# A two-block transformer kernel: stick-breaking sums by a VectorE scan, moved modulations, new allowances

## The chip, the cores and the metric

The kernel runs on one core of a Trainium2 chip. The metric is the device time of one execution in microseconds (us), the median over several runs. Names of engines: PE is TensorE (matrix products and transposes), PEld its weight loads, DVE is VectorE, ACT is ScalarE, POOL is GpSimd, SP is SyncE, whose queue issues the DMA transfers.

## The reference

Two blocks act on x (512 x 1024, fp32). Block 1 puts 16 meta tokens ahead of x, normalises, multiplies by w_in, runs a causal pooling over windows of 2, 4, 8 and 16 tokens and a forgetting attention of 8 heads, merges the two with gates and adds the product with w_out. Block 2 takes c through w_ada to six vectors of 1024 (the modulations: shift, scale and gate of each half), then attention and an MLP. Its attention has 8 stick-breaking heads and 8 chunked heads with relative positions:

```
z = q k^T / 8                         # 128 queries, all keys up to them
strict = s_idx < t_idx
log_1m_beta = where(strict, log_sigmoid(-z), 0)
suffix = cumsum(log_1m_beta, axis=keys, reverse=True) - log_1m_beta
w = where(strict, exp(log_sigmoid(z) + suffix), 0)
out = w @ v
...
mod = silu(c) @ w_ada + b_ada         # sh1, sc1, gt1, sh2, sc2, gt2
x = x + gt1 * (mixed @ w_o)
x = x + gt2 * (square(relu(h @ w1)) @ w2)
```

So the weight of key s for query t is exp(z minus the sum, over keys s to t-1, of softplus(z)).

## The kernel before

Products are made from fp32r parts: each operand is split into a high part (ACT cast, L131) and a low rest (DVE or POOL subtraction, L128), and mm3 (L149 to L152) issues three matmuls for one product. Tiles of weights are 512 KB, loaded raw by SP's queue into the tag wr (5 buffers) and split.

The order of PE's work is set when the program is written. Attention and dense products are generators; weave runs them against each other by a model clock clk and shares of it (SHARE1, SHARE2). After a step, mark or at sets when its result may be used; the allowance is a LAT_ constant in model ns. Other engines follow a scheduler that keeps the written order where data allow it.

The stages, in us of the profiled span: opening with first_norm and the first v products, 0 to 45; weave 1 (attn1 beside dense1: pooling with u_tile at L540 to L565, up-products in ups), 45 to 330; w_out with two joint_norm calls (L711 on) that normalise twice, 330 to 425; the first q, k and v of block 2; the second attention (attn2 beside dense2: v2_chunk, q and k of the pairs, first half of w_o), 443 to 672; the rest of w_o and the norm, to 745; the first MLP half w1 (L1200 to L1308), to 874; the second, w2, to 1055.

The six modulations are made by ada (L203): eight loads of 512 KB each and 16 DVE operations (L215 the first, L217 the rest) that accumulate 128 partial sums. todo holds those still to come, ada_step takes one, and ada_all (L655) takes what is left after weave 1. Modulation 5 is made in the loop of w2, ft 2 to 9.

attn2 goes through pairs of heads in ORDER; p below 4 is a stick-breaking pair, handled by sb_steps with **keys on partitions**: first makes z for one tile of 128 keys and adds a bf16 mask product (L944), then ACT does Abs, Exp, Ln (L946 to L948), DVE does max and addition, giving softplus (L949), a cast (L950) and the rest (L951). second (L963) lets PE add the sums over later keys: a product with the constant ntri (minus ones in a triangle) or nones (minus ones) for each later key tile and for both parts, into the PSUM bank of z. ACT's Exp (L965) gives the weights for pv2 (L916). The chunked pairs, ca_steps, have **queries on partitions**: soft-max on ACT and DVE, PE transposes in turn (L1002), and copies out of PSUM by ACT (L1005) or DVE (L1007) by turns.

```
d0 = min(128 * j2, 256)
pe.matmul(ps[:, d0:], ntri if j2 == j else nones, part[:, SOFF[j2]:SOFF[j2] + 512 - d0],
          start=False, stop=part is sl and j2 == j, skip_group_check=True)
```

Of the kernel before, what the change touches and what calls it, by code (L numbers as in the profile page):

```python
# [51 lines left out]
def hybrid_then_adaln_block(ctx, tc, a, out, tap=None):  # L52
# [96 lines left out]
    def mm3(ps, lh, ll, rh, rl, start, stop):  # L149
        pe.matmul(ps, lh, rh, start=start, stop=False)  # L150
        pe.matmul(ps, lh, rl, start=False, stop=False)  # L151
        pe.matmul(ps, ll, rh, start=False, stop=stop)  # L152
# [1268 lines left out]
```

## Time and profile before

| what | value |
|---|---|
| median of 3 runs | 1059.36 us (1059.28 to 1059.82) |
| profiled execution | 1057.35 us, its span 1055.2 us, mean granted clock 0.994 |
| PE busy | 96% of the span, 5918 instructions |
| DVE, ACT, POOL busy | 60%, 53%, 29% |
| PE stick-breaking sums (L963) | 2% of the chain that ended last |
| DMA | 125.54 MB, 119 GB/s |

The profile is one execution seen by the hardware profiler. Its page gives the busy time of each engine, the waits with what ended them, and groups of instructions by line of the kernel. A time is the start in us from the beginning of the span. A duration of PE is modelled at its end, so the pace of matmuls is read from one start to the next. The granted clock is a share of TensorE's full speed.

### The profile page before, as it was taken

The page shows a single profiled execution, that of the slowest core. Times are in us where ns is not written, and L with a number is a line of the kernel's source. Part 1 is how long each engine was busy: PE and PEld are TensorE (multiplying, and loading weights), DVE is VectorE, ACT ScalarE, POOL GpSimd, SP SyncE. Part 2 cuts the span into 40 slices and gives each one's busy share as a digit, 9 for nine tenths or more (in the row PEclk, how much of TensorE's full clock was granted, in tenths as well). Part 3 has the DMA queues.
Part 4 walks back from the last instruction along what each step waited for, and adds up shares of the span by engine and source line. Part 5 has one row for each costly group of instructions (what it writes and reads, how often), then busy time and mean ns, then how long its engine had stood idle before and what let it go on. Part 6 is the DMA issues. An engine that isn't in the chain of part 4 may idle for free.

```text
span 1055.2 us, 15524 instructions
## 1 busy us (share of the span) xinstructions
PE 1012.8 (96%) x5918; PEld 857.8 (81%) x5918; DVE 628.3 (60%) x1184; ACT 561.8 (53%) x1082; POOL 301.0 (29%) x157
## 2 busy tenths in 40 slices
PE   7999999899999999999899988999999979999998
PEld 5987977768888888987678866799999978888886
DVE  6465866764533669367777476569588862611115
ACT  6365654454545645466687686347567753222220
POOL 3322123423322543203202115122121233233330
PEclk9999999999999999999999999999999999999999
DMA  8442533454543566326421234443234334633302
GB/s 238 126 122 63 154 94 102 138 138 122 149 112 100 181 198 192 128 72 189 126 63 61 68 101 140 146 113 82 66 94 120 121 120 135 177 109 100 100 20 80
DMA packets 136059, 125.54 MB, mean 119 GB/s; under 512 B 8141, under 2 KB 112417, under 8 KB 135986
## 3 DMA queue, kind: packets, MB, share of 16 engines
q1 hardware_dynamic: 135986, 124.56, 40.6%
q8 instruction: 46, 0.75, 0.3%
q14 instruction: 27, 0.22, 0.1%
HBM read 119.82 MB, written 4.73 MB: 118 GB/s over the span
## 4 chain that ended last, share of the span: by engine, by line
PE 76%; DVE 9%; issue 5%; ACT 3%; DMA 3%; POOL 3%; SPq 0%; DVEq 0%; POOLq 0%; ACTq 0%
PE ps L150 19%; PE ps L152 18%; PE ps L151 18%; PE ps L1204 4%; PE ps L1206 3%; PE ps L1205 3%; DVE ada L217 2%; PE ps L963 2%; DMA wr<-in_w_ada_dram 2%; POOL wl L128 1%; DMA wr<-in_w_in_dram 1%; PE ps L519 1%; PE ps L438 1%; PE ps L439 1%; DVE QK L427 1%
## 5 line engine op out<-in xcount | busy, mean ns | idle before, releaser
L128 POOL TENSOR_TENSOR wl<-wr,wh 128x1024 fp32r<-128x1024 f32 x99 | 248.1, 2511 | 577.7 <-ACT wh L131 567.1
L131 ACT CAST wh<-wr 128x1024 fp32r<-128x1024 f32 x130 | 136.3, 1050 | 106.5 <-PE ps L151 55.7
L150 PE MATMUL ps<-hh,wh 128*128 128x512 f32 (+1 forms) x352 | 129.7, 368 | 0.0
L151 PE MATMUL ps<-hl,wh 128*128 128x512 f32 (+1 forms) x352 | 125.1, 355 | 0.0
L152 PE MATMUL ps<-hh,wl 128*128 128x512 f32 (+1 forms) x352 | 124.8, 355 | 0.0
L150 PE MATMUL ps<-wh,T 128*128 128x512 f32 x256 | 101.0, 394 | 0.0
L152 PE MATMUL ps<-wh,T 128*128 128x512 f32 x256 | 100.4, 392 | 0.0
L151 PE MATMUL ps<-wl,T 128*128 128x512 f32 x256 | 100.2, 391 | 0.0
L217 DVE SCALAR_TENSOR_TENSOR ada<-wr,vc,ada 128x512 f32<-128x512 f32 x84 | 81.7, 972 | 11.4 <-DMA wr<-in_w_ada_dram 10.4
L150 PEld LDWEIGHTS ps<-hh,wh 128*128 128x128 f32 x352 | 66.3, 188 | 20.4 <-issue 11.5
L152 PEld LDWEIGHTS ps<-hh,wl 128*128 128x128 f32 x352 | 66.4, 189 | 9.7
L151 PEld LDWEIGHTS ps<-hl,wh 128*128 128x128 f32 x352 | 66.4, 189 | 7.7
L128 DVE TENSOR_TENSOR wl<-wr,wh 128x1024 fp32r<-128x1024 f32 x31 | 41.4, 1336 | 29.1 <-ACT wh L131 29.1
L152 PEld LDWEIGHTS ps<-wh,T 128*128 128x128 f32 x256 | 48.1, 188 | 11.4
L151 PEld LDWEIGHTS ps<-wl,T 128*128 128x128 f32 x256 | 48.1, 188 | 10.7
L150 PEld LDWEIGHTS ps<-wh,T 128*128 128x128 f32 x256 | 48.1, 188 | 10.6
L150 PE MATMUL ps<-h2h,wh 128*128 128x512 f32 (+1 forms) x144 | 54.9, 381 | 0.0
L1206 PE MATMUL ps<-QK,wl 128*128 128x256 f32 x192 | 53.7, 280 | 0.0
L1204 PE MATMUL ps<-QK,wh 128*128 128x256 f32 x192 | 53.7, 279 | 0.0
L1205 PE MATMUL ps<-PT,wh 128*128 128x256 f32 x192 | 53.4, 278 | 0.0
L152 PE MATMUL ps<-h2h,wl 128*128 128x512 f32 (+1 forms) x144 | 53.3, 370 | 0.0
L151 PE MATMUL ps<-h2l,wh 128*128 128x512 f32 (+1 forms) x144 | 53.1, 369 | 0.0
(412 smaller groups left out, 2672.6 us busy)
## 6 DMA issues: line engine op xcount, KB each, us to landing
wr<-in_w_in_dram SPq DMA_DIRECT2D x64, 512.0 KB, 5.8
wr<-in_w_dram SPq DMA_DIRECT2D x64, 512.0 KB, 4.1
wr<-in_w_ada_dram SPq DMA_DIRECT2D x48, 512.0 KB, 4.9
wr<-in_w_out_dram SPq DMA_DIRECT2D x12, 512.0 KB, 3.5
wr<-in_w_o_dram SPq DMA_DIRECT2D x12, 512.0 KB
xr<-in_x_dram SPq DMA_DIRECT2D x8, 512.0 KB
wr<-in_w_up_pool_dram SPq DMA_DIRECT2D x8, 256.0 KB
wr<-in_w_up_attn_dram SPq DMA_DIRECT2D x8, 256.0 KB, 3.3
```

The costliest lines, as they stand in the source:

```text
L128: (eng or pool).tensor_tensor(dst, raw, f(hi), op=OP.subtract)
L131: act.copy(dst_hi, raw)
L150: pe.matmul(ps, lh, rh, start=start, stop=False)
L151: pe.matmul(ps, lh, rl, start=False, stop=False)
L152: pe.matmul(ps, ll, rh, start=False, stop=stop)
L217: dve.scalar_tensor_tensor(acc, raw[:, q, :], cs, acc, op0=OP.mult, op1=OP.add)
L427: dve.scalar_tensor_tensor(A[e][other], src[own], scale, f(A[e][own]), op0=OP.mult, op1=OP.subtract)
L438: pe.matmul(ps, A[e][:, sa], B[e][:, sb], start=True, stop=False)
L963: pe.matmul(ps[:, d0:], ntri if j2 == j else nones, part[:, SOFF[j2]:SOFF[j2] + 512 - d0], start=False, stop=part is sl and j2 == j, skip_ ...
L1204: pe.matmul(ps, wh, bh, start=first and k == 0, stop=False, **go)
L1205: pe.matmul(ps, wh, bl, start=False, stop=False, **go)
L1206: pe.matmul(ps, wl, bh, start=False, stop=k == 3, **go)
```

## The change

- Stick-breaking: sb_steps goes, and so do ntri, nones and the products at L963, the cast and the low rest. att2_steps serves both kinds of pairs with queries on partitions. stick (one unit per 128 queries i and head e, keys 128(i+1)) has the mask turned, Abs, Exp, Ln, max and addition as before, then one DVE scan backward over the keys (a reversed view of the tile; state times one plus the element), the subtraction from z, and Exp in place. Then turn: i+1 PE transposes and one copy, by ACT or DVE by turns. That makes 10 transposes and 4 copies a head.
- attn2: units of a head in the order of i, a lag of three units in place of two, allowances by size for both kinds; LAT_PV2, LAT_QK2, LAT_SQ, LAT_CA and LAT_ADA are longer. pack_a and pack_b change places for q and k.
- Modulation 4 is made in weave 1 (ada_step takes three for m of 4 and more in ups) and no longer after it. ada(5) first copies a column of hid[31], the last tile of w1's result, into its accumulator: the accumulations can only begin behind it.
- u_tile for group 3 (window 16): four additions on DVE in place of POOL.
- Opening: the row of norm_g is loaded ahead of x; 6, 4 and 6 products of ones that nobody reads are put ahead of the first ones.
- v2_chunk: four accumulations in two PSUM banks in place of four.

```
--- before.py
+++ after.py
@@ -34,14 +34,16 @@
 ORDER = (0, 1, 4, 2, 5, 3, 6, 7)
 LAST_SB = 3
 DENSE = (1, "v2", 4, 2, 5, 3, "v3", 6, 7)
-LAT_CA = 5600.0
+LAT_CA = 6000.0
 LAT_SM = 3200.0
-LAT_SB = 4000.0
-LAT_CM = 3200.0
+LAT_SB = (4000.0, 5500.0, 6500.0, 7500.0)
+LAT_CM = (3200.0, 3800.0, 4400.0, 5000.0)
 LAT_QK = 2600.0
-LAT_SQ = 3800.0
-LAT_ADA = 4000.0
+LAT_SQ = 5000.0
+LAT_ADA = 6500.0
 LAT_PV = 600.0
+LAT_PV2 = 1500.0
+LAT_QK2 = 3800.0
...
-    def ada(v, j):
+    def ada(v, j, late=None):
         half, k = j // 4, 2 * (j % 4)
         raw = wts.tile([128, 2, 512], F32, name="wr", tag="wr", bufs=5)
         x = a["w_ada_2"]
@@ -208,6 +210,8 @@
                                   ap=[[6 * D, 128], [128 * 6 * D, 2], [1, 512]]))
         if k == 0:
             ada_acc[0] = consts.tile([128, 512], F32, name="ada", tag="ada", bufs=1)
+            if late is not None:
+                dve.tensor_copy(ada_acc[0][:, :1], late)
         acc = ada_acc[0]
...
+    sp.dma_start(gn, rows(a["norm_g"], 0, 1, D, 0, D))
     sp.dma_start(xr[0], rows(a["x"], 0, 128, D, 0, D))
-    sp.dma_start(gn, rows(a["norm_g"], 0, 1, D, 0, D))
+    idle = bank()
+
+    def warm(n):
+
+        for _ in range(n):
+            pe.matmul(idle[:, :128], ones_f, ones_f, start=True, stop=True)
+
+    warm(6)
...
+    warm(4)
     load_wv(0)
     sp.dma_start(xr[1], rows(a["x"], 128, 128, D, 0, D))
     first_norm(xr[0], 128, NM, *x0)
+    warm(6)
...
         for q in range(g + 1):
             s = wt([128, NP], "T")
-            pool.tensor_tensor(s[:, 2 * w - 1:], prev[:, 2 * w - 1:], prev[:, w - 1:NP - w], op=OP.add)
+            (dve if g == 3 else pool).tensor_tensor(s[:, 2 * w - 1:], prev[:, 2 * w - 1:], prev[:, w - 1:NP - w], op=OP.add)
...
         for m in range(8):
             yield from ups(m)
-            ada_step(2)
-
-    todo += [(v, k) for v in (0, 1, 3) for k in range(8)]
+            ada_step(2 if m < 4 else 3)
+
+    todo += [(v, k) for v in (0, 1, 3, 4) for k in range(8)]
...
     weave((SHARE1, attn1()), (1.0, dense1()))
-    ada_all()
+    assert not todo
...
-    bdt = gated([128, 384], "Cm", late, F32R)
-    bd, nones, ntri = (bdt[:, 128 * q:128 * q + 128] for q in range(3))
+    bd = gated([128, 128], "Cm", late, F32R)
     dve.memset(f(bd), 0.0)
-    dve.tensor_scalar(nones, ones_f, -1.0, None, op0=OP.mult)
...
-    pool.affine_select(mk, mk, pattern=[[1, 128]], base=0, channel_multiplier=-1, compare_op=OP.is_gt, fill=NEG)
+    pool.affine_select(mk, mk, pattern=[[-1, 128]], base=0, channel_multiplier=1, compare_op=OP.is_gt, fill=NEG)
...
-        pss = [bank() for _ in range(4)]
+        pss = [b[:, 256 * q:256 * q + 256] for b in (bank(), bank()) for q in range(2)]
...
-            pack_b(*QK2[p][1:], ps, slice(0, 512), 0.125)
+            pack_a(QK2[p][0], ps, 0.125)
...
-            pack_a(QK2[p][0], ps)
+            pack_b(*QK2[p][1:], ps, slice(0, 512))
...
-            e1 = wt([128, 512], "T")
-            act.activation(e1[:, c0:], ps[:, c0:], AF.Abs)
-            act.activation(e1[:, c0:], e1[:, c0:], AF.Exp, scale=-1.0)
-            act.activation(e1[:, c0:], e1[:, c0:], AF.Ln, bias=1.0)
-            dve.scalar_tensor_tensor(e1[:, c0:], ps[:, c0:], 0.0, e1[:, c0:], op0=OP.max, op1=OP.add)
-            dve.tensor_copy(sh[:, so:so + n], e1[:, c0:])
-            dve.tensor_tensor(sl[:, so:so + n], e1[:, c0:], f(sh[:, so:so + n]), op=OP.subtract)
...
-            for part in (sh, sl):
-                for j2 in range(3, j - 1, -1):
-                    d0 = min(128 * j2, 256)
-                    t += (512 - d0) / 2.4
-                    pe.matmul(ps[:, d0:], ntri if j2 == j else nones, part[:, SOFF[j2]:SOFF[j2] + 512 - d0],
-                              start=False, stop=part is sl and j2 == j, skip_group_check=True)
-            act.activation(WT[:, WOFF[j]:WOFF[j] + n], ps[:, c0:], AF.Exp)
...
+    def att2_steps():
+        def products(p, i, e, stop):
             if i == 0:
-                st[p, e] = (None, None, wt([128, 4, 512], "PT"))
-            bs = strips[2 * (p - 4) + e]
+                st[p, e] = wt([128, 4, 512], "PT"), wt([128, 4, 512], "Y") if p < 4 else None
             L = 128 * (i + 1)
             N = max(L, 256)
             ps = bank()
-            mm_packed(ps[:, :N], QK2[p], e, slice(128 * i, 128 * i + 128), slice(0, N), True)
-            x = P[p, i, e] = wt([128, 512], "T")
+            mm_packed(ps[:, :N], QK2[p], e, slice(128 * i, 128 * i + 128), slice(0, N), stop)
+            x = P[p, i, e] = st[p, e][1][:, i, :] if p < 4 else wt([128, 512], "T")
+            return ps[:, :L], x[:, :L], 2 * N / 2.4
+
+        def stick(p, i, e):
+
+            z, x, t = products(p, i, e, False)
+            pe.matmul(z[:, 128 * i:], identb, mkb, start=False, stop=True)
+            act.activation(x, z, AF.Abs)
+            act.activation(x, x, AF.Exp, scale=-1.0)
+            act.activation(x, x, AF.Ln, bias=1.0)
+            dve.scalar_tensor_tensor(x, z, 0.0, x, op0=OP.max, op1=OP.add)
+            back = x[:, ::-1]
+            dve.tensor_tensor_scan(back, ones_f[:, :1].to_broadcast([128, z.shape[1]]), back, 0.0, op0=OP.mult, op1=OP.add)
+            dve.tensor_tensor(x, z, x, op=OP.subtract)
+            act.activation(x, x, AF.Exp)
+            return t + 56
+
...
             x = P.pop((p, i, e))
-            PT = st[p, e][2]
+            PT = st[p, e][0]
             pt = bank().rearrange("p (j n) -> p j n", j=4)
             for j in range(i + 1):
                 pe.transpose(pt[:, j, :], x[:, 128 * j:128 * j + 128], ident)
...
+        units = [(p, i, e) for p in ORDER for e in range(2) for i in range(4)]
+        LAG = 3
         ripe = {}
         for n in range(len(units) + LAG + 1):
             if n < len(units):
-                kind, *u = units[n]
+                p = units[n][0]
                 if n % 8 == 0:
-                    yield ("qk2", u[0])
-                yield kind[0](*u)
+                    yield ("qk2", p)
+                yield (stick if p < 4 else soft)(*units[n])
                 ada_step()
-                ripe[n] = clk[0] + (LAT_SB if kind is sb else LAT_CM)
+                ripe[n] = clk[0] + (LAT_SB if p < 4 else LAT_CM)[units[n][1]]
                 if n % 8 == 7:
-                    mark(("att", u[0]), 800.0)
+                    mark(("att", p), 800.0)
             if 0 <= n - LAG < len(units):
                 yield at(ripe[n - LAG])
-                yield units[n - LAG][0][1](*units[n - LAG][1:])
+                yield turn(*units[n - LAG])
             m = n - LAG - 1
             if m >= 0 and m % 8 == 7:
-                p = units[m][1]
-                yield at(clk[0] + LAT_PV)
-                yield from pv2(p, [st[p, e][2] for e in range(2)])
+                p = units[m][0]
+                yield at(clk[0] + LAT_PV2)
+                yield from pv2(p, [st[p, e][0] for e in range(2)])
...
-    todo += [(v, k) for v in (4, 2) for k in range(8)]
+    todo += [(v, k) for v in (2,) for k in range(8)]
...
         if 2 <= ft < 10:
-            ada(5, ft - 2)
+            ada(5, ft - 2, hid[31][:, :1])
```

On PE, in the first stick-breaking pair of the second attention. Before (ps PSUM, Y the split softplus, Cm the constants, strip the mask, QK and lz packed q and k, wh and h2h a dense product):

```order
L150 MATMUL ps<-wh,h2h 128x256
L151 MATMUL ps<-wl,h2h 128x256
L152 MATMUL ps<-wh,h2l 128x256
L438 MATMUL ps<-QK 128x256
L439 MATMUL ps<-lz_588,QK 128x256
L944 LDWEIGHTS strip
L944 MATMUL ps<-strip 128x128
L963 MATMUL ps<-Y,Cm 128x256 x2
L963 MATMUL ps<-Y,Cm 128x384
L963 MATMUL ps<-Y,Cm 128x512
```

and now (Y holds the weights, ident the identity):

```order
L987 MATMUL ps<-ident,Y 128x128
L452 MATMUL ps<-QK 128x256
L453 MATMUL ps<-lz_608,QK 128x256
L960 LDWEIGHTS strip
L960 MATMUL ps<-strip 128x128
L152 MATMUL ps<-h2h,wh 128x512
L153 MATMUL ps<-h2l,wh 128x512
L154 MATMUL ps<-h2h,wl 128x512
```

The products of L963 with up to 512 columns are gone; behind each unit's scores stand transposes of 128 columns.

On DVE, in the second joint_norm (jn and jr sums and factors of a row, xr the rows, ada the accumulator of modulation 4). Before:

```order
L728 TENSOR_TENSOR jn_3780<-jn_3780,jn_3781 128x1
L217 SCALAR_TENSOR_TENSOR ada<-wr,vc,ada 128x512
L160 TENSOR_SCALAR rs_t<-rs_y,rs_m 128x1
L217 SCALAR_TENSOR_TENSOR ada<-wr,vc,ada 128x512
L161 SCALAR_TENSOR_TENSOR jr_3782<-rs_t,rs_y 128x1
L725 TENSOR_TENSOR xr<-xr,V 128x512
L730 TENSOR_SCALAR jn_3780<-jn_3780,jr_3782 128x1
L727 TENSOR_TENSOR jn_3817<-jn_3817,jn_3818 128x1
L217 SCALAR_TENSOR_TENSOR ada<-wr,vc,ada 128x512
L157 TENSOR_SCALAR rs_m<-jn_3780 128x1
L728 TENSOR_TENSOR jn_3819<-jn_3819,jn_3820 128x1
```

and now:

```order
L742 TENSOR_TENSOR jn_3838<-jn_3838,jn_3839 128x1
L162 TENSOR_SCALAR rs_t<-rs_y,rs_m 128x1
L163 SCALAR_TENSOR_TENSOR jr_3840<-rs_t,rs_y 128x1
L744 TENSOR_SCALAR jn_3838<-jn_3838,jr_3840 128x1
L739 TENSOR_TENSOR xr<-xr,V 128x512
L159 TENSOR_SCALAR rs_m<-jn_3838 128x1
L741 TENSOR_TENSOR jn_3875<-jn_3875,jn_3876 128x1
L159 TENSOR_SCALAR rs_m<-jn_3875 128x1
L130 TENSOR_TENSOR wl<-wr,wh 128x1024
```

No L217 stands between the steps of the norm; the subtraction of weights (now L130) has moved up among them.

On DVE, at the end of w1 (hid the result, T and wl rests of splits). Before:

```order
L128 TENSOR_TENSOR wl<-T,wh 128x512
L128 TENSOR_TENSOR T<-PT,T 128x512
L217 SCALAR_TENSOR_TENSOR ada<-wr,vc,ada 128x512 x2
L1276 TENSOR_TENSOR hid<-ps,hid 128x256
L1304 TENSOR_TENSOR hid<-ps,hid 128x256
L217 SCALAR_TENSOR_TENSOR ada<-wr,vc,ada 128x512 x2
L1276 TENSOR_TENSOR hid<-ps,hid 128x256
L1304 TENSOR_TENSOR hid<-ps,hid 128x256
```

and now:

```order
L130 TENSOR_TENSOR T<-PT,T 128x512
L1256 TENSOR_TENSOR hid<-ps,hid 128x256
L1284 TENSOR_TENSOR hid<-ps,hid 128x256
L1256 TENSOR_TENSOR hid<-ps,hid 128x256
L1284 TENSOR_TENSOR hid<-ps,hid 128x256
L130 TENSOR_TENSOR wl<-wr,wh 128x1024
L214 COPY ada<-hid 128x1
L284 COPY PTm<-hid 128x1 x2
L219 TENSOR_SCALAR ada<-wr,vc 128x512
L221 SCALAR_TENSOR_TENSOR ada<-wr,vc,ada 128x512 x4
```

The accumulations of modulation 5 (now L219 and L221) stand behind all additions to hid and the copy at L214.

## Rows read from the trace of the kernel before

**Rows 1.** The page, part 1: busy us, share of the span, instructions.
```profile
PE 1012.8 (96%) x5918; PEld 857.8 (81%) x5918; DVE 628.3 (60%) x1184; ACT 561.8 (53%) x1082; POOL 301.0 (29%) x157
```

**Rows 2.** Waits of PE, whole span: total us, times, longest us.
```profile
PE ps L1204 <- DVE hid L1276: 5.4, 1, 5.4
PE ps L360 <- DMA QK<-in_norm_g_dram: 4.6, 1, 4.6
...
PE ps L519 <- ACT PT L504: 3.1, 1, 3.1
...
PE ps L664 <- DVE PTm L733: 2.6, 1, 2.6
```

**Rows 3.** Waits of PE, 443 to 684: the first and last of nine groups.
```profile
PE ps L879 <- DVE PTm L128: 4.6, 4, 1.5
...
PE ps L438 <- DVE QK L427: 0.3, 1, 0.3
```

**Rows 4.** Windows: us, busy of PE, PEld, DVE, ACT, POOL, granted clock, DMA, GB/s.
```profile
443.00:672.00 229.00, 213.89 (x1216) 170.36 (x1214) 154.93 (x344) 156.79 (x334) 48.71 (x33) 0.99 0.36 106
424.00:427.20 3.20, 3.20 (x16) 3.20 (x16) 3.06 (x8) 2.58 (x6) 0.00 (x0) 0.50 0.94 348
864.20:867.40 3.20, 3.12 (x14) 3.12 (x15) 0.36 (x2) 0.78 (x2) 0.00 (x0) 0.50 0.71 230
```

**Rows 5.** Timeline of PE in the second attention: start, us, line, operation.
```profile
470.39 1.45 PE L963 MATMUL ps<-Y,Cm 128*128 128x256 f32 x8
471.68 0.28 PE L150 MATMUL ps<-wh,h2h 128*128 128x256 f32 x1
...
533.13 0.23 PE L944 MATMUL ps<-strip 128*128 128x128 bf16 x1
...
535.97 0.61 PE L1002 MATMUL ps<-ident,T 128*128 128x128 f32 x4
...
536.54 0.28 PE L439 MATMUL ps<-lz,QK 128*128 128x256 f32 x1
...
549.23 0.23 PE L944 MATMUL ps<-strip 128*128 128x128 bf16 x1
```

**Rows 6.** Groups by line, 443 to 672, DVE, then ACT: busy, mean ns.
```profile
L951 DVE TENSOR_TENSOR Y<-T,Y 128x128 fp32r<-128x128 f32 (+3 forms) x32 | 15.7, 490 | 1.1
...
L950 DVE CAST Y<-T 128x128 fp32r<-128x128 f32 (+3 forms) x32 | 14.1, 441 | 1.1
...
L1007 DVE COPY PT<-ps 128x128 f32<-128x128 f32 (+1 forms) x16 | 6.6, 415 | 2.2 <-PE ps L1002 2.1
...
L948 ACT ACTIVATE T<-T 128x128 f32<-128x128 f32 (+3 forms) x32 | 15.1, 473 | 0.4
...
L1005 ACT COPY PT<-ps 128x256 f32<-128x256 f32 (+1 forms) x16 | 7.6, 474 | 7.3 <-PE ps L1002 7.3
```

**Rows 7.** Timeline of DVE at the end of w1.
```profile
858.74 5.15 DVE L217 SCALAR_TENSOR_TENSOR ada<-wr,vc,ada 128x512 f32<-128x512 f32 x2 [0.76 <-DMA wr<-in_w_ada_dram]
863.82 0.41 DVE L1276 TENSOR_TENSOR hid<-ps,hid 128x256 f32<-128x256 f32 x1
```

**Rows 8.** Groups by line and shape, 443 to 672, DVE.
```profile
L949 DVE SCALAR_TENSOR_TENSOR T<-ps,T 128x512 f32<-128x512 f32 x8 | 5.5, 690 | 7.1 <-ACT T L948 7.0
```

**Rows 9.** Timeline of DVE in the second joint_norm.
```profile
412.85 0.74 DVE L217 SCALAR_TENSOR_TENSOR ada<-wr,vc,ada 128x512 f32<-128x512 f32 x1
...
418.87 0.75 DVE L217 SCALAR_TENSOR_TENSOR ada<-wr,vc,ada 128x512 f32<-128x512 f32 x1
```

**Rows 10.** Timeline of DVE behind the additions of u_tile.
```profile
208.76 0.69 DVE L558 SCALAR_TENSOR_TENSOR T<-T 128x512 f32<-128x512 f32 x1 [4.21 <-POOL T L555]
```

**Rows 11.** Timeline of PE in the first v products.
```profile
14.02 0.37 PE L150 MATMUL ps<-Y,hh 128*128 128x256 f32 x1
14.23 0.28 PE L151 MATMUL ps<-Y,hh 128*128 128x256 f32 x1
14.35 0.28 PE L152 MATMUL ps<-Y,hl 128*128 128x256 f32 x1
```

More of the change, by code (lines that the diff above doesn't have):

```diff
@@ L147, in weights, with mm3 @@
         return hi, lo
[L149 to L152, printed above, removed]
+    def mm3(ps, lh, ll, rh, rl, start, stop, **go):
+        pe.matmul(ps, lh, rh, start=start, stop=False, **go)
+        pe.matmul(ps, lh, rl, start=False, stop=False, **go)
+        pe.matmul(ps, ll, rh, start=False, stop=stop, **go)
     def rstd(r, ss, n):
@@ L815, in v2_chunk @@
                     h, l = h_of(k, 128 * t, 128)
-                    mm3(pss[t][:, :256], h, l, wh[:, q, :], wl[:, q, :], k == 0, k == KT - 1)
+                    mm3(pss[t], h, l, wh[:, q, :], wl[:, q, :], k == 0 and t % 2 == 0, k == KT - 1,
+                        skip_group_check=True)
                     yield 325
                 if kk:
-                    act.copy(V2[t][:, 256 * c:256 * c + 256], pss[t][:, :256])
+                    act.copy(V2[t][:, 256 * c:256 * c + 256], pss[t])
     vw = [v2_weights(0), v2_weights(1)]
@@ L915, in pv2 @@
                 hc = slice(128 * p + 64 * e, 128 * p + 64 * e + 64)
-                pe.matmul(po[64 * e:64 * e + 64, 128 * j:], V2[j][:, hc], W[e][:, j, 128 * j:] if p >= 4 else W[e][:, WOFF[j]:WOFF[j] + n],
-                          start=j == 0, stop=j == 3)
+                pe.matmul(po[64 * e:64 * e + 64, 128 * j:], V2[j][:, hc], W[e][:, j, 128 * j:], start=j == 0, stop=j == 3)
             yield 0.89 * n
@@ L928, in hybrid_then_adaln_block @@
     away = []
[L929 to L968 removed]
+    st, P = {}, {}
     strips = {}
@@ L986, in scores, with soft @@
             ps = bank()
-            mm_packed(ps[:, :N], QK2[p], e, slice(128 * i, 128 * i + 128), slice(0, N), True)
-            x = P[p, i, e] = wt([128, 512], "T")
+            mm_packed(ps[:, :N], QK2[p], e, slice(128 * i, 128 * i + 128), slice(0, N), stop)
[13 more added lines that the diff above has]
+            return t + 56
+        def soft(p, i, e):
+            s, x, t = products(p, i, e, True)
             nmx, sums = sm([128, 1], "nmx"), sm([128, 1], "sums")
-            dve.tensor_tensor_reduce(x[:, :L], ps[:, :L], bs[:, 384 - 128 * i:512], scale=-1.0,
-                                     scalar=3.0e38, op0=OP.add, op1=OP.min, accum_out=nmx)
-            act.activation(x[:, :L], x[:, :L], AF.Exp, scale=-1.0, bias=nmx, accum_out=sums)
+            bs = strips[2 * (p - 4) + e]
+            dve.tensor_tensor_reduce(x, s, bs[:, 384 - 128 * i:512], scale=-1.0, scalar=3.0e38,
+                                     op0=OP.add, op1=OP.min, accum_out=nmx)
+            act.activation(x, x, AF.Exp, scale=-1.0, bias=nmx, accum_out=sums)
             dve.reciprocal(sums, sums)
-            dve.tensor_scalar(x[:, :L], x[:, :L], sums, None, op0=OP.mult)
-            return 2 * N / 2.4
+            dve.tensor_scalar(x, x, sums, None, op0=OP.mult)
+            return t
         def turn(p, i, e):
             x = P.pop((p, i, e))
-            PT = st[p, e][2]
+            PT = st[p, e][0]
             pt = bank().rearrange("p (j n) -> p j n", j=4)
@@ L1008, in turn @@
             return 110 * (i + 1)
-        return scores, turn
+        return stick, soft, turn
     def attn2():
         MX[0] = wt([128, 4, 512], "V")
-        sb, ca = sb_steps(), ca_steps()
-        units = []
-        for p in ORDER:
-            if p < 4:
-                units += [(sb, p, j, e) for j in (3, 2, 1, 0) for e in range(2)]
-            else:
-                units += [(ca, p, i, e) for e in range(2) for i in range(4)]
-        LAG = 2
+        stick, soft, turn = att2_steps()
+        units = [(p, i, e) for p in ORDER for e in range(2) for i in range(4)]
+        LAG = 3
         ripe = {}
@@ L1380, in hybrid_then_adaln_block @@
             gt = gtp[5]
-        hs, ws = held[ft]
         if ft < 32 - LAST:
```

34 lines of the change are left out of this document (2 added, 32 removed).

## The prediction

> **What bounds the kernel now.** First the page's part 1: TensorE (PE) is busy 1012.8 of 1055.2 us [rows 1], and no other engine passes 60%. So the sum has two kinds of terms: work taken from PE, and the places where PE still waits, with the half speed that follows some of them. Second the waits of PE over the whole span [rows 2]: the single long ones are a product of the first MLP half on VectorE (DVE) for hid (5.4 us), the opening on the row of norm_g (4.6), attn1 on ScalarE (ACT) for PT (3.1), and joint_norm's transposes on DVE for PTm (2.6). Third the same view cut to the second attention, 443 to 684 us [rows 3]: nine groups from 4.6 down to 0.3 us, 14.8 in all, none of them the old stick-breaking sums. Fourth the windows by stage [rows 4]: in the second attention's 229 us PE is busy 213.9, DVE 154.9 and ACT 156.8, so there PE is the bound and the other two are at 68%.
>
> **Stick-breaking, PE.** The sums run at the pace of [rows 5]: eight products at L963 start at 470.39 and the next work at 471.68. They are the two halves of one key tile, 2 x (256 + 256 + 384 + 512) = 2816 columns, so 0.458 ns a column. A head has four key tiles with 2816, 1792, 1024 and 512 columns, 6144 in all, 2.81 us; eight heads give **-22.5**. In their place stand 10 transposes a head, 80 of 128 x 128. [Rows 5] prices them: four transposes start at 535.97, the 256-column score pair after them at 536.33 and 536.54; transposes and first score product take 0.57, of which 0.12 is a product's own, so 0.113 each and **+9.0**. The score products, the mask product and PV stay as they were. Net **-13.5**. This is the one part that is nearly certain, as PE has no room to hide it in.
>
> **Stick-breaking, the other engines.** DVE loses 32 casts (14.1 us), and gets 16 copies out of the transposes (6.6, as its present 16) and 32 scans; ACT gets the other 16 copies (7.6) [rows 6]. No scan is in this trace. Below, it costs what the subtraction beside it costs, 0.49 us a piece, 15.7 in all; a scan that only reads and writes such a tile can hardly be under that. Above, the slowest row of DVE on such tiles: an accumulation of 512 elements at 2.6 us [rows 7], scaled to the mean of 320 elements 1.6 us, 52 in all. I take the lower end, since the operand shapes are those of the subtraction. [...]
> DVE then has 154.9 - 14.1 + 6.6 + 15.7 = 163 us, less some 6 of accumulations that go to an earlier stage, and ACT 164, in about 213 us: 74 to 77%. What releases PE is a chain. For 512 keys it is seven operations on ACT or DVE behind the mask product (Abs, Exp, Ln, the DVE operation at L949 that takes 0.69 [rows 8], the scan, the subtraction, Exp): at about that each 4.8 us, or 6.7 with the upper scan. The new allowance is 7.5 for that size, four for 128 keys, and three units lie between a score product and its transpose, so I expect no new wait at most heads. The waits of 14.8 shrink, as every allowance in this stage grows: term **-3**, with bounds of -12 (nearly all gone) and +9 (a new wait at each of the six points where DVE and ACT meet bursts, each as long as the longest here, 1.5).
>
> **Modulation 4 goes to weave 1.** Six accumulations of 0.74 or 0.75, the first at 412.85 and the last at 418.87, leave DVE's chain through the second joint_norm [rows 9]; at its end stands the normalising at L733, for whose PTm PE waits 2.6 us [rows 2]. [...] **-4.2**, bounds 0 (the subtraction of w_out's weights, which stands in the same chain on DVE, is late next) and -4.2. Its 16 accumulations and 4 MB of loads are added at the end of weave 1: 12 us of DVE at 0.74, with SP's queue carrying eight more loads of 512 KB ahead of those of w_out. They lie beside PE's up-products; if a load is late PE waits about a landing time. I cost it at nothing.
>
> **Modulation 5 waits for hid.** DVE's accumulation at 858.74 takes 5.15 for two, and the addition for hid at 863.82 (0.41) stands behind it [rows 7]; PE waits 5.4 us at L1204 [rows 2], and then 3.2 us run at 0.50 [rows 4]. With the gate these accumulations come behind the last addition. 5.4 less the 0.4 of the addition itself, and 1.6 of the clock: **-6.6**, bounds -4 and -7. The 16 accumulations land in the second MLP half, where DVE has hardly any work; five buffers of raw weights hold two of them longer, which can make a weight load of that half late.
>
> **u_tile's additions on DVE.** GpSimd (POOL) does them beside its subtractions of weights; DVE's next step, at 208.76, waits 4.21 for them [rows 10], ACT stands behind that, and PE waits 3.1 for ACT's PT [rows 2]. DVE is idle for most of that wait, and does such an addition in about the 0.69 of that next step, so what is left is the one just before it. **-2.5**, bounds 0 and -3.1.
>
> **Opening.** The idle products keep PE busy before the first transposes, and norm_g's row goes first: the wait of 4.6 [rows 2]. After it the 256-column products follow each other by 0.21 us up to 14.23 and by 0.12 from there [rows 11]; ten at the faster pace are 0.9 less. But the whole opening follows weights and x that DMA is still bringing, so **-1**, bounds +0.5 and -3.
>
> v2_chunk on two banks, the new gates and the LAT numbers for modulations add no PE work; their cover is the same PE queue. **Sum**: -13.5 - 3 - 4.2 - 6.6 - 2.5 - 1 = -30.8. The profiled execution took 1057.35, which gives 1026.5; the median of the runs is 2.0 above it, so **1028.5** beside 1059.36.
>
> **Rivals.** *One: DVE and ACT become the bound in bursts.* A stick pair's first and last mask products lie 16.1 us apart (533.13 and 549.23 [rows 5]); less sums and plus transposes, 5.6 and 2.3, that becomes 12.7. ACT is asked for four passes over each of eight units, 15.1 us at the 0.473 of L948, and now for four copies of 0.474 [rows 6]: 17.0, of which 7/8 or 14.9 between these two products. For: the burst is longer than PE's time, and the first pair has modulation 2 on DVE besides. Against: a lack of 2.2 us is less than the 2.7 by which the allowance exceeds the chain, and over the stage both stay at 77%. Were each of four stick pairs late by 3 us: 1040. *Two: the single waits are replaced.* Removing one lets the next thing come late (w_out's weights at joint_norm, a weight load of the second MLP half, attn1's next ACT pass); only -13.5 and -3 stay: 1043. *Three, on the other side: the scan runs element by element.* DVE without scans has some 141 us in the stage; it becomes the bound once the scans pass 70 us, 2.2 a piece, and the other gains are eaten at 3.2 a piece, over six times the subtraction; at 4.0 the stage takes 270 us and the kernel 1085. Nothing in the trace is that slow on such a tile. *Four: the idle products do not raise the pace*: the opening's 1 us is lost, 1029.5.
>
> **Chances.** Forecast with rival four 0.58; rival one 0.26; rival two 0.09; rival three 0.05, and 0.02 for any that balance out. All upper gains together (-13.5 - 12 - 4.2 - 7 - 3.1 - 3 = -42.8) give 1014.5 to 1016.5, by whether the runs lie above the profiled one as they do now; rivals one and two end at 1043. Range 1014 to 1043. 0.2%, 2.1 us, is about what can be told from no change here: faster 0.93, same 0.02, slower 0.05.
>
> **What would show it.** L963 gone and 80 more transposes at 0.11; PE about 999 us busy. Scans of about 0.7 us at 512 elements; over 1.2 would put rival one ahead. No wait of PE above 1 us at the transposes of Y; no row of PE on hid above 1 us; none on PTm at joint_norm; no clock of 0.50 around 424 and 864. I am wrong if the second attention shrinks by less than 10 us, or if DVE's idle time there falls under 20 us.

## The result, and the profile after

The changed kernel takes 1035.28 us (median of 4 runs, 1033.05 to 1038.12) beside 1059.59 for the kernel before, a ratio of 0.977 (95% interval 0.9744 to 0.9795). The forecast was 1028.5: the sign and the range (1014 to 1043) held, and the gain is 24 us in place of 31. The profiled execution took 1035.2 with a span of 1033.5, 21.7 less than before. Part 1 of its page, beside [rows 1]:

```profile
PE 999.8 (97%) x5870; PEld 850.0 (82%) x5870; DVE 654.9 (63%) x1204; ACT 567.1 (55%) x1098; POOL 294.5 (28%) x136
```

PE is busy for 13.0 us less; DVE and ACT do more, as forecast. The gain by stages is read from the starts of the same products in both traces. The last column is what the stretch up to that point gained or lost.

| point | before, us | after, us | stretch before it |
|---|---|---|---|
| first score of attn1 | 64.0 | 65.4 | **+1.4** |
| last transpose of the second joint_norm | 425.1 | 423.3 | **-3.2** |
| last PV product of the second attention | 670.3 | 655.6 | **-12.9** |
| end | 1055.2 | 1033.5 | **-7.0** |

The -7.0 lies in w1: its last product starts at 873.5 before and at 851.7 after, and w2 behind it takes the same time.

The waits of PE over the whole span (total us, times, longest), beside [rows 2]:

```profile
PE ps L453 <- DVE lz L448: 4.4, 1, 4.4
PE ps L152 <- ACT V L828: 3.3, 3, 1.9
PE ps L238 <- DVE Y L967: 2.5, 1, 2.5
PE ps L515 <- DVE T L504: 2.4, 1, 2.4
...
PE ps L678 <- DVE PTm L747: 0.6, 1, 0.6
```

Of the four long waits of before, the one on hid is gone, the one on PTm is down to 0.6, and the one in attn1 has a new name (on DVE's T in place of ACT's PT). The one on norm_g's row in the opening is no longer listed: the idle products run in its place, and the product behind it starts at 4.09 us in place of 4.63. The three largest now lie in the second attention, which had 14.8 us of waits [rows 3] and now has 18.2 (441 to 670).

### The profile page after: what moved, and what is told of

Same layout as the page of the kernel before. It is cut to its first block, busy times and chain, and to the rows that moved or that the text cites. A ratio compares the mean times of both kernels' runs of the same rounds, so it can differ in the third digit from the quotient of the medians.

```text
span 1033.5 us, 15410 instructions
## 1 busy us (share of the span) xinstructions
PE 999.8 (97%) x5870; PEld 850.0 (82%) x5870; DVE 654.9 (63%) x1204; ACT 567.1 (55%) x1098; POOL 294.5 (28%) x136
## 4 chain that ended last, share of the span: by engine, by line
PE 83%; DVE 7%; ACT 5%; issue 3%; POOL 1%; DMA 1%; DVEq 0%; POOLq 0%; ACTq 0%
PE ps L152 21%; PE ps L153 20%; PE ps L154 20%; PE ps L1184 4%; PE ps L1186 4%; PE ps L1185 4%; PE ps L987 2%; PE ps L923 1%; PE ps L452 1%; PE ps L453 1%; DVE ada L221 1%; PE ps L533 1%; PE ps L515 1%; PE ps L238 1%; DVE Y L966 1%
## 5 line engine op out<-in xcount | busy, mean ns | idle before, releaser
L130 POOL TENSOR_TENSOR wl<-wr,wh 128x1024 fp32r<-128x1024 f32 x99 | 247.4, 2502 | 616.9 <-ACT wh L133 611.7
L221 DVE SCALAR_TENSOR_TENSOR ada<-wr,vc,ada 128x512 f32<-128x512 f32 x84 | 83.0, 988 | 6.4 <-DMA wr<-in_w_ada_dram 5.1
L152 PEld LDWEIGHTS ps<-hh,wh 128*128 128x128 f32 x352 | 66.3, 188 | 19.7 <-issue 10.8
L154 PEld LDWEIGHTS ps<-wh,T 128*128 128x128 f32 x256 | 48.1, 188 | 10.8
L152 PEld LDWEIGHTS ps<-wh,T 128*128 128x128 f32 x256 | 48.1, 188 | 10.6
L130 DVE TENSOR_TENSOR wl<-wr,wh 128x1024 fp32r<-128x1024 f32 x31 | 40.9, 1319 | 24.1 <-ACT wh L133 24.0
```

Source lines behind the costliest of these rows:

```text
L130: (eng or pool).tensor_tensor(dst, raw, f(hi), op=OP.subtract)
L152: pe.matmul(ps, lh, rh, start=start, stop=False, **go)
L154: pe.matmul(ps, ll, rh, start=False, stop=stop, **go)
L221: dve.scalar_tensor_tensor(acc, raw[:, q, :], cs, acc, op0=OP.mult, op1=OP.add)
```

## The experiments

All runs stand beside the kernel before on their own chip; the stage is the second attention, from the last transpose of joint_norm to the last PV product, in the run's profile.

| run | ratio (95% interval) | span | stage |
|---|---|---|---|
| changed kernel | 0.977 (0.9744 to 0.9795) | 1033.5 | 232.3 |
| e1 modulation 2 late | 0.9823 (0.9808 to 0.9837) | 1038.5 | 236.4 |
| e2 no scan | 0.9734 (0.9719 to 0.9748) | 1028.3 | 229.9 |
| e3 last idle products out | 0.9814 (0.9789 to 0.984) | 1035.1 | 233.7 |
| e4 old sums, old allowances | 0.992 (0.9907 to 0.9932) | 1046.6 | 246.7 |
| e5 modulation 2 spread | 0.9774 (0.976 to 0.9787) | 1029.4 | 231.5 |
| e6 four banks | 0.9782 (0.9764 to 0.98) | 1036.5 | 236.6 |
| e7 pooling on POOL | 0.9804 (0.9785 to 0.9823) | 1032.2 | 232.5 |
| e8 old opening | 0.9799 (0.9785 to 0.9814) | 1032.7 | 235.7 |
| e9 longer allowances | 0.9772 (0.9749 to 0.9795) | 1032.4 | 232.8 |
| e10 scan, old allowances | 0.9894 (0.9874 to 0.9914) | 1044.6 | 245.6 |
| e11 modulations 4, 5 back | 0.989 (0.9875 to 0.9904) | 1043.6 | 235.7 |
| e12 old sums, new allowances | 0.9776 (0.9762 to 0.979) | 1034.9 | 234.5 |

The changed kernel's own runs lie 5 us apart, and a difference of 2 us between two of these kernels is not told from none by the times. The stage is read from one profile of each kernel, and it scatters too: the changed kernel, e3, e7 and e8 have the same code there and take 232.3, 233.7, 232.5 and 235.7. So a difference of under 3.4 us in the stage is not told from none either.

### Scan and allowances: e4, e10, e12

The change puts two things into one stage, a scan for PE's sums and longer allowances. e4 is the kernel before with every other part of the change. The order of units goes with the way of summing: it is the old one in e4 and e12 and the new one in e10.

```
# e4: before.py with these parts of the change, and no other
+ warm(6), warm(4), warm(6); norm_g's row ahead of x
+ ada_step(2 if m < 4 else 3); todo (0, 1, 3, 4), then (2,); ada(5, ft - 2, hid[31][:, :1])
+ (dve if g == 3 else pool) in u_tile; two banks in v2_chunk
```

> Edit: the kernel before with all other parts of the change (opening, modulations 4 and 5, pooling on DVE, two banks in v2_chunk), but stick-breaking by PE products, and attn2 with its old allowances. Theory sum of parts: the second attention has its 227 us again and the rest is as in the changed kernel, about 1045 to 1047. If the new allowances and the order of units, not the work taken from PE, gave the gain of that stage, nothing else would show it here; if two banks in v2_chunk cost several us, the stage is longer than before by that, 1048 to 1050.

```
# e10: after.py
-LAT_CA = 6000.0; LAT_SQ = 5000.0; LAT_ADA = 6500.0; LAT_PV2 = 1500.0; LAT_QK2 = 3800.0
+LAT_CA = 5600.0; LAT_SQ = 3800.0; LAT_ADA = 4000.0; LAT_PV2 = 600.0; LAT_QK2 = 2600.0
-LAT_SB = (4000.0, 5500.0, 6500.0, 7500.0); LAT_CM = (3200.0, 3800.0, 4400.0, 5000.0); LAG = 3
+LAT_SB = (4000.0,) * 4; LAT_CM = (3200.0,) * 4; LAG = 2
```

> Edit: the allowances and the lag of the kernel before (4.0 for stick-breaking, 3.2 for chunked units, a lag of two and so on), with the scan. Theory allowances carry it: the chain of 512 keys needs some 5.5 us with the scan, so transposes wait 1 to 2 us at many of the 32 units, the stage is 10 us or more longer, 1043 to 1050. Theory allowances hardly matter: within 3 us, 1035 to 1038.

```
# e12: e4 with the change's allowances and lag
-ripe[n] = clk[0] + (LAT_SB if kind is sb else LAT_CM); LAG = 2
+ripe[n] = clk[0] + (LAT_SB[3 - u[1]] if kind is sb else LAT_CM[u[1]]); LAG = 3
+LAT_SB, LAT_CM, LAT_CA, LAT_SQ, LAT_ADA, LAT_PV2, LAT_QK2 as in after.py
```

> Edit: the run with the old stick-breaking sums, given the new allowances by size, the lag of three and the longer PV and score allowances; the fourth corner beside the changed kernel (scan, new allowances), the run with old allowances (scan) and the run with the old sums (old allowances). Theory needs both (the scan's work only pays where the allowances cover its longer chain, and the old sums had few waits to save): the second attention has 243 to 247 us from the last transpose of the second joint_norm, as with the old allowances, kernel 1046 to 1050. Theory allowances alone: they take 8 to 13 us off here too, the stage has 234 to 239 us, kernel 1037 to 1042, and the scan's own part is only some 3 to 5 us.

The four corners, by the stage:

| | old allowances | new allowances |
|---|---|---|
| sums on PE | e4 246.7 | e12 234.5 |
| scan | e10 245.6 | changed kernel 232.3 |

**The allowances, with the lag, take 12.2 us off with the old sums and 13.3 with the scan; the scan takes off 1.1 and 2.2, which is less than the scatter of the stage.** The times say the same: by the ratios the allowances are worth some 15 and 13 us and the scan some 3 and under 1; e12 has the ratio of the changed kernel within both intervals, e10 nearly that of e4. e12 bears out the theory that the allowances do it alone, e10 that they carry the scan. Which of the allowances does it, or the lag, no run takes apart. Two times lie outside what their theory said: e12 (1034.2) is below its 1037 to 1042, and e4 (1049.3) lies in the 1048 to 1050 that its text gave to two slow banks, with a stage 1.5 us longer than before; e6 below shows no cost of the banks.

The changed kernel has 11.7 us less busy time on PE than e12, and e10 11.3 less than e4. Where that went is seen in the windows of the stage and of the first two stick-breaking pairs, 444 to 492 (us; busy PE, PEld, DVE, ACT, POOL; granted clock; DMA, GB/s). The kernel before:

```profile
425.10:670.30 245.20, 231.42 (x1358) 188.13 (x1357) 161.38 (x357) 165.33 (x350) 53.79 (x37) 0.99 0.35 104
444.00:492.00 48.00, 47.67 (x312) 40.23 (x311) 31.55 (x66) 30.80 (x72) 6.79 (x9) 1.00 0.42 120
```

e4, old sums and old allowances:

```profile
421.20:667.90 246.70, 229.91 (x1351) 186.70 (x1350) 157.79 (x348) 165.69 (x350) 54.02 (x37) 0.99 0.31 94
```

e12, old sums and new allowances:

```profile
422.80:657.30 234.50, 225.73 (x1351) 185.41 (x1350) 155.37 (x349) 165.34 (x350) 54.09 (x37) 1.00 0.33 98
444.00:492.00 48.00, 45.71 (x292) 38.11 (x292) 38.55 (x71) 32.92 (x73) 13.45 (x9) 1.00 0.50 143
```

The changed kernel:

```profile
423.30:655.60 232.30, 215.11 (x1272) 175.31 (x1269) 170.12 (x365) 171.64 (x366) 55.11 (x21) 0.98 0.33 100
444.00:492.00 48.00, 38.22 (x239) 31.77 (x238) 42.15 (x74) 33.43 (x78) 12.13 (x4) 0.93 0.50 143
```

e10, the scan with old allowances:

```profile
420.70:666.30 245.60, 219.44 (x1272) 175.78 (x1270) 172.71 (x365) 170.75 (x366) 52.43 (x21) 0.97 0.32 94
```

Over the stage the changed kernel has 10.6 us less busy time on PE than e12 (215.1 beside 225.7) and 8.4 more idle time. Of that, 7.5 lies in these 48 us, where PE is idle for 9.8 in place of 2.3; the clock of 0.93, beside a whole one in e12, takes another 3.4, which is inside the busy time. So most of the work taken from PE came back as waiting and slow clock inside the first two pairs, while DVE is busy for 42.2 of 48 us (31.6 before, 38.6 in e12). With the old allowances e10 loses 26 us of its stage to idle PE, and the largest waits in sum are now at the transposes of the new steps:

```profile
PE ps L987 <- ACT Y L968: 5.6, 7, 1.5
PE ps L453 <- DVE lz L448: 5.4, 1, 5.4
```

### The first pairs: e1, e2, e5, e9

What stands on DVE in the first stick-breaking pair of the changed kernel (start, us, line):

```profile
445.68 0.42 DVE L966 TENSOR_TENSOR_SCAN Y<-ones_f,Y 128x128 f32<-128x128 f32 x1
...
446.66 0.28 DVE L967 TENSOR_TENSOR Y<-ps,Y 128x128 f32<-128x128 f32 x1
...
447.85 0.68 DVE L966 TENSOR_TENSOR_SCAN Y<-ones_f,Y 128x256 f32<-128x256 f32 x1
...
450.56 0.95 DVE L966 TENSOR_TENSOR_SCAN Y<-ones_f,Y 128x384 f32<-128x384 f32 x1
...
453.79 1.22 DVE L966 TENSOR_TENSOR_SCAN Y<-ones_f,Y 128x512 f32<-128x512 f32 x1
454.93 2.79 DVE L221 SCALAR_TENSOR_TENSOR ada<-wr,vc,ada 128x512 f32<-128x512 f32 x1
457.64 0.68 DVE L967 TENSOR_TENSOR Y<-ps,Y 128x512 f32<-128x512 f32 x1
```

The scan (L966) takes 0.42, 0.68, 0.95 and 1.22 us for 128 to 512 elements: (1.22 - 0.42) / 384 = 2.08 ns an element, where the subtraction (L967) goes from 0.28 to 0.68, 1.04 an element. Between scan and subtraction stand modulation 2's accumulations (L221), one of which takes 2.79 us in place of 0.73. A second one takes 2.76, again just ahead of the subtraction, and then of lz, a packed part of q or k, which L448 makes at 471.52:

```profile
468.04 2.76 DVE L221 SCALAR_TENSOR_TENSOR ada<-wr,vc,ada 128x512 f32<-128x512 f32 x1
470.73 0.68 DVE L967 TENSOR_TENSOR Y<-ps,Y 128x512 f32<-128x512 f32 x1
```

Both run beside a subtraction of weights on POOL, which ends 0.5 us before them (start, us):

```profile
454.74 2.43 POOL L130 TENSOR_TENSOR wl<-wr,wh 128x1024 fp32r<-128x1024 f32 x1 [43.02 <-ACT wh L133]
466.26 4.00 POOL L130 TENSOR_TENSOR wl<-wr,wh 128x1024 fp32r<-128x1024 f32 x1 [9.09 <-ACT wh L133]
```

And PE's two long waits end right behind them, the first by the profile on that subtraction of DVE (L967), the second on lz:

```profile
458.37 1.05 PE L238 MATMUL ps<-ones_f,ada 128*128 128x1 f32 x8 [2.51 <-DVE Y L967]
...
472.25 0.58 PE L453 MATMUL ps<-lz,QK 128*128 128x256 f32 x1 [4.44 <-DVE lz L448]
```

Four runs ask what of this holds PE. e2 puts a plain multiplication in place of the scan and so leaves out the sums over later keys.

```
# e1                                      # e5
-ada_step()                               -ada_step()
+if n >= 16: ada_step()                   +if n % 4 == 3: ada_step()
# e2
-dve.tensor_tensor_scan(back, ones, back, 0.0, op0=OP.mult, op1=OP.add)
+dve.tensor_tensor(back, ones, back, op=OP.mult)
# e9: e5, and
+LAT_SB = (6000.0, 7500.0, 8500.0, 9500.0); LAT_QK2 = 6500.0
```

> Edit: modulation 2's steps start at unit 16 of the second attention instead of unit 0, so the first stick-breaking pair has DVE for itself. Theory queue (DVE is full in the first stick pair because scans and modulation 2 meet there): the waits of PE on the subtraction behind the scan (2.5 us) and on lz (4.4 us) and the slow clock behind them go, the second attention gets 5 to 9 us shorter, kernel about 1027 to 1030. Theory scan alone (DVE would be full there without modulation 2 as well): under 2 us, about 1034. Theory banks (v2_chunk's two banks hold PE): no change in that stretch, 1035.

> Edit: the scan is replaced by a plain multiplication by ones of the same shape, so the sums over later keys are left out. Theory scan alone: DVE loses some 13 us (0.89 to 0.49 a piece) and most of the new waits of the first pair, the kernel gets 5 us or more shorter, under 1030. Theory queue: modulation 2 still stands between the steps, 2 to 4 us shorter, 1031 to 1033. Theory banks: no change, 1035.

> Edit: modulation 2's steps are taken at every fourth unit of the second attention, so one load and two accumulations meet four units, in place of one each unit. Theory queue (it is the meeting of accumulations and scans in one burst that holds PE): the waits on lz and behind the subtraction go as in the run with late steps, and no later pair gets a burst in their place, so the second attention is 4 to 8 us shorter than in the changed kernel, 1028 to 1031. Theory no net gain (DVE's work is late wherever it is put, and the slow clock follows every wait): 1034 to 1038, with the waits in other places.

> Edit: modulation 2's steps at every fourth unit, and 2 us more allowance for every stick-breaking unit (6.0 to 9.5) and 2.7 us more before a pair's first score. Theory late results (the first pair's results come 2 to 4 us later than the allowance says, and dense products are there to fill it): the waits on lz and on the subtraction go, 4 to 6 us off the second attention, 1028 to 1030. Theory conserved (DVE and ACT deliver the pairs at their own pace, and dense products put in early are missing at the end): waits reappear near 600 to 650, 1032 to 1036.

Windows as above, e1:

```profile
422.90:659.30 236.40, 219.69 (x1271) 176.60 (x1270) 173.61 (x365) 171.89 (x366) 54.16 (x21) 0.96 0.32 98
444.00:492.00 48.00, 43.74 (x257) 35.09 (x256) 36.63 (x59) 35.66 (x82) 7.17 (x3) 0.93 0.12 34
```

e2:

```profile
420.50:650.40 229.90, 214.62 (x1272) 174.95 (x1269) 160.78 (x365) 170.79 (x366) 52.43 (x21) 0.98 0.34 101
444.00:492.00 48.00, 41.50 (x255) 33.95 (x255) 37.24 (x74) 35.68 (x80) 12.15 (x5) 0.93 0.50 143
```

e5:

```profile
419.10:650.60 231.50, 216.34 (x1272) 174.39 (x1270) 169.15 (x363) 170.48 (x366) 51.67 (x21) 0.98 0.33 100
444.00:492.00 48.00, 42.65 (x258) 34.45 (x258) 37.62 (x63) 33.93 (x77) 7.98 (x4) 0.96 0.30 88
```

e1 is a miss of the queue theory: the wait on lz fell from 4.4 to 1.1, the one of 2.5 is gone from the first pairs (one of 1.6 on the same line of DVE comes at 538.28), PE was busy for 43.7 us there in place of 38.2, and yet the stage became 4.1 us longer and the ratio higher, with intervals apart. The accumulations then met pairs 4 and 2: from 492 to 560 PE is busy for 62.5 us in e1 and for 67.6 in the changed kernel, and the clock of the stage fell to 0.96. Spread over the stage (e5) they cost little there and won little: 0.8 us in the stage, the same ratio. Without the scan's extra time (e2) the stage is 2.4 us shorter and the ratio lower by 0.36%, 3.8 us, with intervals that just meet: nearer to the 2 to 4 us of the queue theory than to the 5 and more of the scan alone, but not clear of the scatter. Still longer allowances (e9) change nothing: 232.8.

So DVE's load in the first pairs is part of what holds PE, shown by e1, e2 and e5, each of which raises PE's busy time there (43.7, 41.5 and 42.7 us beside 38.2); but none of these edits makes the kernel clearly shorter. The two long waits go with the two slow accumulations: in e6, e7 and e8 one of 2.79 stands ahead of a wait of 2.5 and one of about 2.8 ahead of a wait on lz of 2.9 to 4.4; in e2 one of 2.85 stands ahead of a wait on lz of 3.6; where none is slow there (e1, e5, e9, e11) the first wait is missing and the one on lz is at most 1.6. Against it, e3 has the first of the two pairs, but behind its second slow stretch (two accumulations in 4.28) no wait on lz, and e12 has one accumulation of 2.90 and two of 3.02 together in the same 48 us with no wait above 1.1. That POOL's subtraction makes the two waits is therefore argued, not shown; no run moves it. What else is in the 5 to 7 us of idle time left in e2 and e5 (DVE busy for 37.2 and 37.6), beside 2.3 in e12 with 38.6, stays open.

### The other parts: e3, e6, e7, e8, e11

```
# e3
 first_norm(xr[0], 128, NM, *x0)
-warm(6)
# e8: no warm at all, and
-sp.dma_start(gn, ...); sp.dma_start(xr[0], ...)
+sp.dma_start(xr[0], ...); sp.dma_start(gn, ...)
```

> Edit: the last six idle products of the opening, ahead of the first v product, are left out. Theory in the way (they run 2.4 us on PE just where the first v products could start): the first transposes stay where they are, weave 1 starts 1 to 2 us earlier, kernel 1 to 2 us shorter. Theory warm (they pay back by the faster pace of the products behind them): the first ten v products take 0.21 us each again and weave 1 starts at the same time or later, no change or +1.

> Edit: the opening of the kernel before (no idle products, norm_g's row behind x). Theory bound by loads: weave 1 starts within 1 us of the changed kernel's 65.4 us, the ratio to the kernel before is that of the changed kernel within its interval. Theory gain as forecast: it starts 1 us later. Theory in the way: it starts 1.4 us earlier, at the 64.0 of the kernel before.

The first v product of the kernel before (start, us, line), beside [rows 11]:

```profile
11.95 0.56 PE L150 MATMUL ps<-Y,hh 128*128 128x256 f32 x1
```

The changed kernel's opening on PE (start, us, line, count of parts):

```profile
11.37 2.62 PE L303 MATMUL ps<-ones_f 128*128 128x128 f32 x12
13.75 0.37 PE L152 MATMUL ps<-Y,hh 128*128 128x256 f32 x1
```

and e3's:

```profile
11.40 0.58 PE L152 MATMUL ps<-Y,hh 128*128 128x256 f32 x1
...
14.90 0.39 PE L153 MATMUL ps<-Y,hh 128*128 128x256 f32 x1 [1.21 <-POOL Y L130]
```

The faster pace came: behind the first v product they follow each other by 0.12 us from 13.95 on, where before they took 0.21 up to 14.23. But the last idle products run until 13.75, so the first one starts 1.8 us later than before. Without them (e3) it does start at 11.40, and the pace is 0.12 from 12.36 on; but then PE waits for POOL's rests of w_in at 14.90, and attn1's first score comes at 65.5 (65.4 in the changed kernel). In the profiles both theories fall: the idle products are neither in the way nor do they pay back. e8 has the first score at 63.9, as before; over all runs with the new opening it comes between 63.8 and 65.4. In e3 the start is held by the splits, and the idle products won nothing that the starts show. The ratios of e3 and e8 are higher by 0.4 and 0.3% with intervals that overlap the changed kernel's, so a gain of the forecast 1 us is not excluded either.

```
# e7
-(dve if g == 3 else pool).tensor_tensor(s[:, 2 * w - 1:], ...)
+pool.tensor_tensor(s[:, 2 * w - 1:], ...)
```

> Edit: the additions of u_tile for group 3 are on GpSimd again. Theory replaced wait (DVE's additions hold the division of the softmax, 2.4 us, in place of the 3.1 on PT): weave 1 has the same length within 1 us, kernel 1034.5 to 1036.5. Theory gain as forecast: 2.5 us longer, 1038.

DVE in weave 1 of the changed kernel, beside [rows 10]:

```profile
204.37 3.23 DVE L569 TENSOR_TENSOR T<-T 128x525 f32<-128x525 f32 x2
...
208.05 0.48 DVE L504 TENSOR_SCALAR T<-T,sums 128x528 f32<-128x528 f32 x1
```

POOL beside it:

```profile
203.92 2.38 POOL L130 TENSOR_TENSOR wl<-wr,wh 128x1024 fp32r<-128x1024 f32 x1 [8.06 <-ACT wh L133]
```

So POOL subtracts weights from 203.92 to 206.30. Two of the four additions took 3.23 us there, and the division of a softmax (L504), for which PE waits 2.4, stands behind them. In e7 PE waits 2.7 for PT at 211.02. From the first score of attn1 to the last transpose of joint_norm e7 has 356.9 us and the changed kernel 357.9, e3 357.9 and e5 354.7: a replaced wait, with no gain that this stretch shows. But e7's profile is the fastest of its four runs (1034.0; median 1037.9), and its ratio is higher by 0.3%, 3.6 us, with intervals that overlap: the times neither show the forecast gain of 2.5 nor exclude it.

```
# e6
-pss = [b[:, 256 * q:256 * q + 256] for b in (bank(), bank()) for q in range(2)]
+pss = [bank()[:, :256] for _ in range(4)]
... (and the start flags of mm3 as in before.py)
```

> Edit: v2_chunk accumulates in four banks again. Theory banks: the waits of PE on the copies of v2_chunk (3.3 us in three) go and the slow clock behind the largest with them, 3 to 5 us shorter, 1030 to 1032. Theory free list: the two banks that v2_chunk no longer takes are what the third unit of lag lives on, so other waits for banks take the place, 1035 or longer.

The waits on v2_chunk's copies (3.3 us) are gone, and the ratio is the same. In 444 to 492 the clock is 0.82, the waits on the subtraction (2.5) and on lz (2.9) stay, and the stage is 236.6, in a profile that is the slowest of its four runs. Neither theory can be told from these times.

```
# e11
-ada_step(2 if m < 4 else 3); todo (0, 1, 3, 4); assert not todo; todo (2,); ada(5, ft - 2, hid[31][:, :1])
+ada_step(2); todo (0, 1, 3); ada_all(); todo (4, 2); ada(5, ft - 2)
```

> Edit: modulation 4 is made after weave 1 again and modulation 5 no longer waits for hid. Theory of the forecast: the wait before the transposes of the second joint_norm and the wait on hid at the end of w1 come back with their slow clock, 4.2 and 6.6 us, 1045 to 1047. If either wait had gone by other means (the scan, the opening), that part of it does not come back: 1039 to 1042.

Waits of PE in e11, and the windows at those on PTm and hid:

```profile
PE ps L154 <- DVE wl L130: 6.1, 1, 6.1
...
PE ps L1184 <- DVE hid L1256: 5.2, 1, 5.2
PE ps L678 <- DVE PTm L747: 2.6, 1, 2.6
```

```profile
420.00:424.00 4.00, 3.19 (x16) 3.19 (x16) 3.46 (x7) 1.39 (x3) 0.00 (x0) 0.58 0.82 316
852.00:856.00 4.00, 2.79 (x13) 2.79 (x14) 1.48 (x3) 0.63 (x1) 0.27 (x1) 0.50 0.43 143
```

Both waits are back at their old size with a clock of 0.58 and 0.50 there. From the last PV to the end e11 has 384.1 us, the kernel before 384.9, the changed kernel 377.9. The ratio rises by 1.2%, 12.7 us, a little over the 10.8 expected. Not all of it is the two waits: the end takes 6.2 us more than in the changed kernel, the stretch up to joint_norm 2.1 more, and the stage 3.4 more. Half of modulation 4 is then made in the stage again, and the longest wait of e11, the 6.1 us, ends there at 496.13. Ahead of it on DVE a scan takes 3.37 us and a subtraction of weights 3.29, beside two subtractions of POOL.

## Why the prediction was right or wrong, by its steps

- **Stick-breaking on PE, -13.5, "nearly certain".** The work left PE nearly as priced: 11.7 us of busy time from e12 to the changed kernel, 11.3 from e4 to e10. The step that failed is the next one, that PE has no room to hide it in and so the stage must follow: with the allowances held the scan is worth 1.1 to 2.2 us of the stage (e4 and e10, e12 and the changed kernel), within the scatter. A busy share of 93% in [rows 4] left 15 us of waits for the stage to shrink or grow by.
- **Allowances, -3.** This term was mis-sized: 12.2 and 13.3 us, at its bound of -12. In e12 PE's idle time in the stage is 8.8 us, in e4 16.8, and the granted clock of the stage goes from 0.99 to 1.00.
- **The sum of both, -16.5,** against -12.9 measured, came near since one error covers the other. That is luck, and so is part of how near the total came. By stretches the span was to lose 30.8 us and lost 21.7: this stage 3.6 less than forecast, the stretch up to joint_norm 3.5 less (-4.2 and -2.5 against -3.2), the opening 2.4 less, the end 0.4 more.
- **The scan at 0.49 us, the lower end.** It takes 0.89 in the mean (28.5 us for 32), and 0.42 to 1.22 by its size where nothing slows it. The 1.22 at 512 elements is just over the 1.2 that by the prediction's own sign would put rival one ahead. An element costs it 2.08 ns, against 1.04 for the subtraction behind it (L967). Without its extra time (e2) the stage is 2.4 us shorter, which is within the scatter.
- **Rival one, DVE and ACT in bursts.** It came in the first two of the four stick pairs, where modulation 2 is made: by the windows of e12 and the changed kernel 7.5 us of idle time and 3.4 of slow clock, 10.9 in all. It was priced at 12 over all four and given a chance of 0.26. That two of DVE's accumulations take 2.79 and 2.76 us there, in place of 0.73, was not in it.
- **Joint_norm, -4.2.** It was priced as the wait of 2.6 [rows 2] and half of the 3.2 us at a clock of 0.50 behind it [rows 4], 1.6; that half is an estimate, which no run shows by itself. The wait fell from 2.6 to 0.6 and the clock in 424 to 427.2 rose from 0.50 to 1.00: the mechanism is right. By the starts it is -3.2, but that stretch holds all of weave 1 and takes 354.7 to 358.3 us in the runs with this part (361.1 before), so the size is not read closer than that.
- **Hid, -6.6.** -7.0 by the starts, of which e11 gives 6.2 back. Right.
- **u_tile, -2.5.** The step that failed is the cost of an addition, and the wait was replaced as in rival two: I took the additions at 0.69 because DVE was idle; two of them took 3.23 beside POOL's subtraction, ahead of a softmax step, and PE waits 2.4 there in place of 3.1. What is left of the gain stays open (e7). Four slow stretches of DVE in this trace (204.37, 454.93, 468.04 and 498.01) end 0.5 to 1.3 us after a subtraction of POOL; that it makes them is not shown.
- **Opening, -1.** Wrong in sign in the changed kernel's profile (+1.4), and nothing over the runs (63.8 to 65.4 beside 64.0). The faster pace came, against rival four; the step that failed is that the products would start as early as before.
- **All parts but the stick-breaking stage, -14.3.** e4, which has just these, is 0.8% or 8.5 us under the kernel before. By the starts in its trace that is +1.3 in the opening, -5.2 up to joint_norm, +1.5 in the stage and -6.2 at the end.
- **The median above the profiled run by 2.0.** Here they agree within 0.1.

## What to carry to other kernels

Here work taken from the busiest engine, 11.3 and 11.7 us, hardly shortened its stage, by 1.1 and 2.2, as what feeds it did not deliver sooner. When a change also loosens the due times of an order written by hand, run the four corners before the gain is put down to either: here the due times alone give the same time within the scatter, with PE's old work still in place. An operation of unknown speed is better priced at the slow end when the engine that runs it has a full stretch ahead of it.
